# 88 instead of 96 gathered tokens in an expert layer: the last 24 in groups of 16 and 8, 40 tokens' gate table on chip

## The chip, the core and the metric

The kernel runs on one core of a Trainium2 chip, in one launch. The metric is device time in microseconds (us), the median of three runs. A core has a matrix engine (PE, with its weight loads shown apart as PEld), a vector engine (DVE), an activation engine (ACT), GpSimd (POOL) and SyncE (SP). SP, ACT and POOL each issue transfers on a queue of their own, and all queues are served by the same 16 DMA engines.

## The reference, cut to what matters

Two blocks of a network run over 256 tokens of 2048 channels in float32. The change touches the last part, a layer of 16384 experts with one hidden neuron each:

```python
def peer(h, w_q, sub_keys, u_tab, v_tab):          # u_tab, v_tab: 16384 x 2048
    q = (xb @ w_q).reshape(tokens, 8, 2, 128)
    s = einsum('thcd,hcnd->thcn', q, sub_keys)
    ...                                            # 8 heads, 16 experts each
    expert, gates = top16_of_pair_sums(s), softmax(best)
    u_sel, v_sel = u_tab[expert], v_tab[expert]
    act = gelu(einsum('td,thkd->thk', xb, u_sel))
    return einsum('thk,thkd->td', gates * act, v_sel)
```

Behind it come a residual addition and a normalization of each token's row. Each token uses 128 of the 16384 experts.

## The kernel before

**Two ways for the experts.** The 256 tokens are split. 160 tokens go *densely* through all experts: 128 tiles of 128 experts, 1 MB of `u` and 1 MB of `v` a tile. A u-step (`u_step`, products on L1517) multiplies 16 pieces of a u tile with the tokens' columns, 128x160 each, and ACT stores the gelu (L1520). A v-step (`v_step`, `v_products`, L1534) adds 16 products of the v tile with these activations to sums that stay in the accumulator banks 2 to 7. Each float32 product is two instructions on PE, so that a step is 32 of them. The other 96 tokens go *sparsely*: three groups of 32 tokens are spread over the 128 partitions in four quarters (a quarter holds 32 of a token's 128 experts), and an indirect DMA on POOL (`gather`, L1388) fetches one expert's row per partition, 1 MB a gather, 192 gathers in all. On DVE a u item (L1416) multiplies the rows with the tokens (`x_rep`) and sums them; ACT makes the gelu of four such sums at a time (L1434); a v item (L1431) adds the weighted rows to `acc_s`. The quarters are written to DRAM (`sd`), read back and added at the end.

**Order.** 58 u-steps come first, then v-steps and u-steps in turn (70 of each), then 58 v-steps, of which the last two are done by banks, with the closing normalization. The dense tiles come through a ring of five buffers (with three more at its start); SP loads a tile as soon as a buffer is free. The gathers have a ring of five buffers, too, and POOL issues the next when DVE has used one. The program text is written step by step, and each engine follows it in order: after each step `run_paced` adds 0.82 sparse items to the text (`pace`). Each engine may run ahead of the others as far as data and buffers allow. Three things tie them: ACT's gelu of four sparse sums stands in ACT's order between the evacuations of u-steps; the loads of `xq` (`xd` in DRAM to the buffers 20 and 21, L1568 to L1571) stand in POOL's order behind the last u-step, which still reads these buffers; and `weigh` on DVE (L1366, L1369) puts the gates on a tile's activations up to two v-steps ahead.

**The gates.** While the last u-steps run, `gbuild` makes the table of gates for the dense tokens, four tokens at a time (L1350, four products of 128x128). Blocks of 16 tokens are written to DRAM (`gd`, eight blocks), two stay on chip (`kept`). `gload` brings the gates of 16 expert tiles back at a time, 1 MB.

**Handing out.** When the first 128 tokens' choice is known, `hand_out(0)` spreads the expert numbers over the partitions (`rbuf`, L1237), `sp_start` starts the first five gathers, and `hand_out(1)` spreads the gates.

## Time and profile before

| | us |
|---|---|
| median of three runs | 2521.33 |
| lowest, highest | 2519.53, 2522.07 |
| the profiled execution, its own time | 2517.49 |
| span of its trace, first to last instruction | 2515.5 |
| PE, PEld, DVE, ACT, POOL busy | 2395.5, 2268.2, 1604.3, 696.9, 663.0 |
| mean granted clock of PE | 0.99 |

The expert layer takes the last 1290 us of the span. The times of a row are us from the span's start; a busy PE is not PE at its peak, since its instructions overlap.

### The profile page before, as it was taken

How to read it: one execution, taken by the hardware profiler on the slowest of the kernel's cores; microseconds unless marked ns; L12 is line 12 of the kernel's file. 1: busy time of each engine (PE TensorE's matmuls, PEld its weight loads, DVE VectorE, ACT ScalarE, POOL GpSimd, SP SyncE). 2: the span in 40 equal slices, each digit the busy share in tenths (PEclk: the TensorE clock that was granted, in tenths of full speed). 3: DMA queues.
4: the chain of work that ended last, by engine and by line, in shares of the span. 5: the costliest groups of instructions: out<-in, count | busy, mean ns of one | idle time of the engine just before them, and what ended most of it. 6: DMA issues, size and time to landing. Idle time of an engine off the chain costs nothing.

```text
span 2515.5 us, 40335 instructions
## 1 busy us (share of the span) xinstructions
PE 2395.5 (95%) x16832; PEld 2268.2 (90%) x16832; DVE 1604.3 (64%) x2643; ACT 696.9 (28%) x1043; POOL 663.0 (26%) x855
## 2 busy tenths in 40 slices
PE   8999999999999999999999998999999899999997
PEld 7888888899999999988999998988988889999886
DVE  6857777589999987657778675434454343425433
ACT  5544454443335345454211560000000000000002
POOL 1788888410000000140121113212112232121110
PEclk9999999999999999999999999999999999999998
DMA  6455555565555544555599999999999999999994
GB/s 238 168 200 185 176 193 201 203 240 213 198 203 184 185 168 170 187 213 183 217 384 420 420 391 361 413 391 421 417 421 417 385 422 417 390 367 420 418 370 159
DMA packets 110997, 737.76 MB, mean 293 GB/s; under 512 B 13248, under 2 KB 15456, under 8 KB 25280
## 3 DMA queue, kind: packets, MB, share of 16 engines
q1 hardware_dynamic: 65760, 474.50, 49.6%
q0 software_dynamic: 36064, 237.62, 23.7%
q10 hardware_dynamic: 8992, 23.07, 2.5%
q8 instruction: 132, 2.16, 0.3%
q14 instruction: 49, 0.40, 0.0%
HBM read 704.90 MB, written 27.00 MB: 291 GB/s over the span
## 4 chain that ended last, share of the span: by engine, by line
PE 69%; DMA 25%; DVE 4%; ACT 1%; issue 0%; SPq 0%; DVEq 0%; ACTq 0%
DMA s<-in_vexp_dram 14%; PE b L1517 14%; PE b L293 14%; PE b L1534 11%; DMA s<-in_wst_dram 9%; PE b L294 7%; PE b L278 4%; PE b L280 4%; PE b L279 4%; PE b L271 2%; PE b L423 2%; PE b L270 2%; PE b L269 2%; DVE s L195 2%; PE b L1350 1%; PE b L897 1%
## 5 line engine op out<-in xcount | busy, mean ns | idle before, releaser
L1534 PE MATMUL b<-s,s 128*128 128x160 f32 x4096 | 585.2, 303 | 49.7 <-DMA s<-in_vexp_dram 37.3
L1534 PEld LDWEIGHTS b<-s,s 128*128 128x128 f32 x4096 | 566.1, 192 | 66.2 <-issue 49.9
L1517 PE MATMUL b<-s,s 128*128 128x160 f32 x4096 | 584.0, 301 | 27.5 <-DMA s<-in_wst_dram 25.0
L1517 PEld LDWEIGHTS b<-s,s 128*128 128x128 f32 x4096 | 563.5, 191 | 40.0 <-issue 35.9
L293 PE MATMUL b<-s,s 128*128 128x512 f32 x1680 | 597.9, 399 | 0.0
L294 PE MATMUL b<-s,s 128*128 128x256 f32 x1680 | 471.7, 281 | 9.1 <-DVE s L195 9.0
L195 DVE TENSOR_TENSOR s<-s,s 128x2048 fp32r<-128x2048 f32 x192 | 452.3, 2358 | 26.8 <-issue 12.5
L293 PEld LDWEIGHTS b<-s,s 128*128 128x128 f32 x1680 | 315.9, 188 | 71.4
L1416 DVE CUSTOM_DVE_ANT_0 s<-s,s 128x2048 f32<-128x2048 f32 x96 | 219.7, 2290 | 251.5 <-DMA s<-in_uexp_dram,rbuf 224.6
L189 ACT ACTIVATE s<-s 128x2048 fp32r<-128x2048 f32 x192 | 365.7, 1906 | 9.9 <-DMA s<-in_wst_dram 9.9
L294 PEld LDWEIGHTS b<-s,s 128*128 128x128 f32 x1680 | 317.7, 189 | 13.3 <-DVE s L195 12.5
L1431 DVE SCALAR_TENSOR_TENSOR s<-s,sqsum,s 128x2048 f32<-128x2048 f32 x93 | 218.5, 2349 | 164.1 <-DMA s<-in_vexp_dram,rbuf 163.6
L1520 ACT ACTIVATE s<-b 128x160 f32<-128x160 f32 x128 | 38.4, 300 | 825.3 <-PE b L1517 819.6
L278 PE MATMUL b<-s,s 128*128 128x256 f32 x896 | 256.6, 286 | 0.0
L280 PE MATMUL b<-s,s 128*128 128x256 f32 x896 | 253.6, 283 | 0.0
L279 PE MATMUL b<-s,s 128*128 128x256 f32 x896 | 253.5, 283 | 0.0
L1388 POOL DMA_INDIRECT s<-in_uexp_dram,rbuf x96 | 119.8, 1248 | 393.0 <-DVE s L1431 237.2
L1388 POOL DMA_INDIRECT s<-in_vexp_dram,rbuf x96 | 110.2, 1148 | 411.8 <-DVE sqsum L1416 269.6
L278 PEld LDWEIGHTS b<-s,s 128*128 128x128 f32 x896 | 171.8, 192 | 3.7 <-issue 2.9
L279 PEld LDWEIGHTS b<-s,s 128*128 128x128 f32 x896 | 171.9, 192 | 0.3
L280 PEld LDWEIGHTS b<-s,s 128*128 128x128 f32 x896 | 171.9, 192 | 0.0
L837 POOL TENSOR_TENSOR sqsum<-sqsum,s 128x256 f32<-128x256 f32 x28 | 57.9, 2066 | 385.6 <-ACT s L835 385.5
(303 smaller groups left out, 2461.9 us busy)
## 6 DMA issues: line engine op xcount, KB each, us to landing
s<-in_wst_dram SPq DMA_DIRECT2D x320, 1024.0 KB, 5.3
s<-in_vexp_dram SPq DMA_DIRECT2D x128, 1024.0 KB, 19.1
tabd<-s POOLq DMA_DIRECT2D x32, 256.0 KB, 4.7
s<-tabd ACTq DMA_DIRECT2D x32, 256.0 KB, 3.5
gd<-s ACTq DMA_DIRECT2D x8, 1024.0 KB, 11.4
s<-gd POOLq DMA_DIRECT2D x6, 1024.0 KB, 28.9
xd<-s POOLq DMA_DIRECT2D x4, 1024.0 KB, 9.8
s<-in_bblk_dram ACTq DMA_DIRECT2D x8, 512.0 KB, 4.0
```

What stands on the lines that cost most here:

```text
L189: nc.scalar.activation(hi_of(i), raw_of(i), AF.Copy)
L195: nc.vector.tensor_tensor(out=lo_of(i), in0=raw_of(i), in1=FV(hi_of(i)), op=ALU.subtract)
L278: nc.tensor.matmul(ps, a, xh, start=(j == 0), stop=False)
L279: nc.tensor.matmul(ps, a, xl, start=False, stop=False)
L280: nc.tensor.matmul(ps, b, xh, start=False, stop=(j == len(perm) - 1))
L293: nc.tensor.matmul(ps, a, x2, start=(j == 0), stop=False)
L294: nc.tensor.matmul(ps[:, :T], b, x2[:, :T], start=False, stop=(j == len(perm) - 1))
L1388: nc.gpsimd.indirect_dma_start(out=gb[m % len(gb)][0:n, :], out_offset=None, in_=uexp if kind == "u" else vexp, in_offset=bass.IndirectOff ...
L1416: V.tensor_tensor_reduce(out=buf, in0=buf, in1=x_rep[0:4 * n, :], scale=1.0, scalar=0.0, op0=ALU.mult, op1=ALU.add, accum_out=dots_[:, k:k ...
L1431: V.scalar_tensor_tensor(out=ac, in0=buf, scalar=a, in1=ac, op0=ALU.mult, op1=ALU.add)
L1517: nc.tensor.matmul(ps, raw[:, k * P:(k + 1) * P], nv(k)[:, NS_:T], start=(k == 0), stop=(k == KT - 1))
L1534: nc.tensor.matmul(acc[d], raw[:, d * P:(d + 1) * P], act_at(i), start=False, stop=(i == P - 1 and (d % 3 == 2 or d == KT - 1)))
```

## The change

Eight tokens move from the gathered to the dense way: 88 are gathered, 168 are dense. The gathered tokens are now in groups of 32, 32, 16 and 8, all on 128 partitions: a token of the third group has eight parts of 16 experts, one of the fourth sixteen parts of 8, so that the last groups take 32 and 16 gathers; in all there are 176. `pace` is 0.78. The dense products are 128x168. The gate table has 42 pieces of four tokens; eight blocks still go to DRAM, and 16, 16 and 8 tokens stay on chip, so that `weigh` has three small products in place of two.

The parts of the last two groups are no longer written to DRAM: `join_rows` multiplies `acc_s` with a matrix of ones and zeros (`sel`) on PE, four products of 512 columns a group in two pairs, into the banks 0 and 1, and DVE adds them to the residual rows, which are read early (`y_rows`). The numbers and gates of these groups go over a small list in DRAM (`li16`, `li8`), since a token's experts now spread over more partitions. The gathers start after the first group's numbers are handed out.

```diff
 NEG = -1e30
-GROUPS = [(0, 32), (32, 32), (64, 32)]
-NS_ = 96
+GROUPS = [(0, 32), (32, 32), (64, 16), (80, 8)]
+NS_ = 88
 NT = T - NS_
...
         self.paced = []
-        self.pace, self.paced_credit = 0.82 * 2350, 0
+        self.pace, self.paced_credit = 0.78 * 2350, 0
         self.credit = 0
...
     xrow = drp.tile([NS_, D], F32, name="xrow")
-    sd = drp.tile([4, NS_, D], F32, name="sd")
-    NSP = NT // 16 - 2
+    sd = drp.tile([4, 64, D], F32, name="sd")
+    lists = [drp.tile([P, 2, n], F32, name=f"li{n}") for _, n in GROUPS[2:]]
+    NSP = 8
+    STAY = [16, 16, 8]
+    assert 16 * NSP + sum(STAY) == NT
     gd = drp.tile([NSP, P, P, 16], F32, name="gd")
...
             V.tensor_copy(abr[:, P:2 * P], flat(gat))
-        for g, (t0, n) in enumerate(GROUPS):
-            for q in range(4):
-                nc.gpsimd.dma_start(rbuf[n * q:n * q + n, 64 * g + 32 * c:64 * g + 32 * c + 32],
-                                    abr[t0:t0 + n, P * c + 32 * q:P * c + 32 * q + 32])
-        if c == 0:
-            sp_start()
+        for g in range(2):
+            hand_to(c, g)
+            if c == 0 and g == 0:
+                sp_start()
+        for g in range(2, len(GROUPS)):
+            hand_to(c, g)
+    def hand_to(c, g):
+        t0, n = GROUPS[g]
+        Q = P // n
+        K = P // Q
+        dst = rbuf[:, LCOL[g] + c * K:LCOL[g] + c * K + K]
+        if g < 2:
+            for q in range(Q):
+                nc.gpsimd.dma_start(dst[n * q:n * q + n], abr[t0:t0 + n, P * c + K * q:P * c + K * q + K])
+            return
+        li = lists[g - 2]
+        nc.gpsimd.dma_start(li.rearrange("(q t) c k -> t c q k", t=n)[:, c],
+                            abr[t0:t0 + n, P * c:P * c + P].rearrange("p (q k) -> p q k", q=Q))
+        nc.gpsimd.dma_start(dst, li[:, c])
...
+    def by_expert(n):
+        return stage(n).rearrange("p (i t) -> p i t", i=P)
     def gbuild():
-        kept.extend(slots([9]) + [stg[0]])
+        kept.extend(slots([9]) + [stg[0], S[24][:, 0:8 * P]])
         for t4 in range(NT // 4):
...
         n = t4 // 4
-        sg = stage(n).rearrange("p (i t) -> p t i", t=16)
+        sg = by_expert(n).rearrange("p i t -> p t i")
         for q in range(4):
...
         if t4 % 4 == 3 and n < NSP:
-            nc.scalar.dma_start(gd[n], stage(n).rearrange("p (i t) -> p i t", t=16))
+            nc.scalar.dma_start(gd[n], by_expert(n))
...
         nc.vector.tensor_tensor(out=a3, in0=a3, in1=gblk(i // 16)[:, :, i % 16, :], op=ALU.mult)
-        for n in range(2):
-            r = a[:, 16 * (NSP + n):16 * (NSP + n) + 16]
-            nc.vector.tensor_tensor(out=r, in0=r, in1=kept[n][:, 16 * i:16 * i + 16], op=ALU.mult)
+        t0 = 16 * NSP
+        for n, w in enumerate(STAY):
+            r = a[:, t0:t0 + w]
+            nc.vector.tensor_tensor(out=r, in0=r, in1=by_expert(NSP + n)[:, i, :], op=ALU.mult)
+            t0 += w
         if i % 16 == 15 and i // 16 + 2 < 8:
...
+    batches = [(g, k) for g, (_, n) in enumerate(GROUPS) for k in range(0, n, 4)]
     items = []
-    for j in range(8 * len(GROUPS) + 1):
-        for kind, n in (("u", j), ("v", j - 1)):
-            if 0 <= n < 8 * len(GROUPS):
-                items += [(kind, n // 8, n % 8 * 4 + k) for k in range(4)]
+    for j in range(len(batches) + 1):
+        for kind, m in (("u", j), ("v", j - 1)):
+            if 0 <= m < len(batches):
+                items += [(kind, batches[m][0], batches[m][1] + k) for k in range(4)]
     gb = []
+    DCOL = [0, 32, 64, 80]
...
         kind, g, k = items[m]
-        n = 4 * GROUPS[g][1]
         nc.gpsimd.indirect_dma_start(
-            out=gb[m % len(gb)][0:n, :], out_offset=None, in_=uexp if kind == "u" else vexp,
-            in_offset=bass.IndirectOffsetOnAxis(ap=gaddr[0:n, 64 * g + k:64 * g + k + 1], axis=0))
+            out=gb[m % len(gb)][:], out_offset=None, in_=uexp if kind == "u" else vexp,
+            in_offset=bass.IndirectOffsetOnAxis(ap=gaddr[:, LCOL[g] + k:LCOL[g] + k + 1], axis=0))
...
         t0, n = GROUPS[g]
-        for q in range(4):
+        for q in range(P // n):
             nc.gpsimd.dma_start(x_rep[n * q:n * q + n, :], S[18][t0:t0 + n, :])
...
             yield None
-        late = []
+        V.memset(sel, 0.0)
+        for g, (t0, n) in list(enumerate(GROUPS))[2:]:
+            V.tensor_reduce(out=sel[:, 96 * (g - 2) + t0:96 * (g - 2) + t0 + n],
+                            in_=ident.rearrange("p (q t) -> p t q", t=n), axis=AX.X, op=ALU.add)
+        late, sums = [], []
+        acc_s = None
         for m, (kind, g, k) in enumerate(items):
             t0, n = GROUPS[g]
-            buf = gb[m % len(gb)][0:4 * n, :]
-            dots_, acts = dots[0:4 * n, 32 * g:32 * g + 32], dots[0:4 * n, P + 32 * g:P + 32 * g + 32]
+            buf = gb[m % len(gb)]
+            dots_, acts = [dots[:, o + DCOL[g]:o + DCOL[g] + n] for o in (0, P)]
             if kind == "u":
-                V.tensor_tensor_reduce(out=buf, in0=buf, in1=x_rep[0:4 * n, :], scale=1.0, scalar=0.0,
+                V.tensor_tensor_reduce(out=buf, in0=buf, in1=x_rep, scale=1.0, scalar=0.0,
                                        op0=ALU.mult, op1=ALU.add, accum_out=dots_[:, k:k + 1])
...
                 if k % 4 == 0:
-                    a4 = acts[:, k:k + 4]
-                    V.tensor_tensor(out=a4, in0=a4, in1=rbuf[0:4 * n, 64 * g + 32 + k:64 * g + 36 + k], op=ALU.mult)
+                    a4, o = acts[:, k:k + 4], LCOL[g] + n + k
+                    V.tensor_tensor(out=a4, in0=a4, in1=rbuf[:, o:o + 4], op=ALU.mult)
                 if g == 0 and k == 0:
                     acc_s = slots([10])[0]
-                ac = acc_s[0:4 * n, :]
                 if k == 0:
-                    V.tensor_scalar(ac, buf, a, None, op0=ALU.mult)
+                    V.tensor_scalar(acc_s, buf, a, None, op0=ALU.mult)
                 else:
-                    V.scalar_tensor_tensor(out=ac, in0=buf, scalar=a, in1=ac, op0=ALU.mult, op1=ALU.add)
+                    V.scalar_tensor_tensor(out=acc_s, in0=buf, scalar=a, in1=acc_s, op0=ALU.mult, op1=ALU.add)
             while late and m >= late[0][0]:
...
                 gather(m + len(gb))
-            if kind == "u" and k == 31 and g < len(GROUPS) - 1:
+            if kind == "u" and k == n - 1 and g < len(GROUPS) - 1:
                 rows(g + 1)
-            if kind == "v" and k == 31:
-                for q in range(4):
-                    nc.gpsimd.dma_start(sd[q, t0:t0 + n, :], acc_s[n * q:n * q + n, :])
+            if kind == "v" and k == n - 1:
+                if g < 2:
+                    for q in range(4):
+                        nc.gpsimd.dma_start(sd[q, t0:t0 + n, :], acc_s[n * q:n * q + n, :])
+                else:
+                    sums.append((m + 3, g))
+            if sums and m == sums[0][0]:
+                yield 2350
+                yield from join_rows(sums.pop(0)[1], acc_s)
             yield 2350
-        parts = [s[0:NS_, :] for s in gb]
+        y = y_rows[0]
+        quarters = [gb[q][0:64, :] for q in range(4)]
         for q in range(4):
-            nc.gpsimd.dma_start(parts[q], sd[q])
-        nc.gpsimd.dma_start(parts[4], xrow)
-        for _ in range(5):
+            nc.gpsimd.dma_start(quarters[q], sd[q])
+        for _ in range(3):
             yield None
-        for q in range(1, 5):
-            V.tensor_tensor(out=parts[0], in0=parts[0], in1=parts[q], op=ALU.add)
+        yield from join_rows(sums.pop(0)[1], acc_s)
+        for q in range(4):
+            V.tensor_tensor(out=y[0:64, :], in0=y[0:64, :], in1=quarters[q], op=ALU.add)
             yield 2350
...
         c = small[0:NS_, 40:50]
-        nc.scalar.activation(parts[1], parts[0], AF.Square, accum_out=c[:, 0:1])
-        V.tensor_tensor(out=parts[0], in0=parts[0], in1=gf[0:NS_, :], op=ALU.mult)
+        nc.scalar.activation(gb[0][0:NS_, :], y, AF.Square, accum_out=c[:, 0:1])
+        V.tensor_tensor(out=y, in0=y, in1=gf[0:NS_, :], op=ALU.mult)
         yield 2350
...
         yield None
-        nc.scalar.activation(parts[0], parts[0], AF.Copy, scale=c[:, 3:4])
-        nc.gpsimd.dma_start(out[0:NS_, :], parts[0])
+        nc.scalar.activation(y, y, AF.Copy, scale=c[:, 3:4])
+        nc.gpsimd.dma_start(out[0:NS_, :], y)
+    sel, u_done = rconv, [False]
+    y_rows = []
+    def join_rows(g, acc_s):
+        t0, n = GROUPS[g]
+        assert u_done[0]
+        if not y_rows:
+            y_rows.append(slots([18])[0][0:NS_, :])
+            nc.gpsimd.dma_start(y_rows[0], xrow)
+        s_ = sel[:, 96 * (g - 2):96 * (g - 2) + NS_]
+        for h in range(2):
+            for c in range(2):
+                nc.tensor.matmul(B[c][0:NS_, :], s_, acc_s[:, (2 * h + c) * 512:(2 * h + c + 1) * 512],
+                                 start=True, stop=True)
+            yield None
+            for c in range(2):
+                r = y_rows[0][64:NS_, (2 * h + c) * 512:(2 * h + c + 1) * 512]
+                nc.vector.tensor_tensor(out=r, in0=r, in1=B[c][64:NS_, :], op=ALU.add)
+            yield 1400
```

POOL before, behind the first gathers of the start (`rbuf` holds numbers and gates by partition): the gates of all three groups are handed out in 12 transfers, and the gathers go on.

```order
L1388 DMA s_11237<-in_uexp_dram,rbuf 128x2048
L1388 DMA s_11238<-in_uexp_dram,rbuf 128x2048
L1237 DMA rbuf<-s_10073 32x32 x12
L1388 DMA s_11234<-in_uexp_dram,rbuf 128x2048
L1388 DMA s_11235<-in_uexp_dram,rbuf 128x2048
L1388 DMA s_11236<-in_uexp_dram,rbuf 128x2048
```

The same place in the change (L1413 is the gather; `li_10085` and `li_10086` are the lists):

```order
L1413 DMA s_11232<-in_uexp_dram,rbuf 128x2048
L1254 DMA rbuf<-s_10073 32x32 x4
L1257 DMA li_10085<-s_10073 16x8x16
L1259 DMA rbuf<-li_10085 128x16
L1257 DMA li_10086<-s_10073 8x16x8
L1259 DMA rbuf<-li_10086 128x8
L1254 DMA rbuf<-s_10073 32x32 x8
L1257 DMA li_10085<-s_10073 16x8x16
L1259 DMA rbuf<-li_10085 128x16
L1257 DMA li_10086<-s_10073 8x16x8
L1259 DMA rbuf<-li_10086 128x8
L1413 DMA s_11228<-in_uexp_dram,rbuf 128x2048
```

Four lists now stand between the fifth and the sixth gather, each read back right behind its write. Over the whole of POOL's order 42 gathers stood ahead of the instruction that opens the dense sums, 115 between it and the `xq` loads, and 35 behind these; now they are 41, 109 and 26.

PE before, at a v-step of the last stretch (`b_67` to `b_72` are the banks of the dense sums, `s_10972` activations, `s_80` and `s_10975` tiles of v):

```order
L1534 MATMUL b_72<-s_10972,s_80 128x160
L1534 MATMUL b_67<-s_10972,s_10975 128x160 x3
L1534 MATMUL b_68<-s_10972,s_10975 128x160 x3
L1534 MATMUL b_69<-s_10972,s_10975 128x160 x3
L1534 MATMUL b_70<-s_10972,s_10975 128x160 x3
L1534 MATMUL b_71<-s_10972,s_10975 128x160 x3
L1534 MATMUL b_72<-s_10972,s_10975 128x160
```

In the change, behind the 100th v-step (`s_11660` is `acc_s`, `rconv` holds `sel`):

```order
L1591 MATMUL b_72<-s_10974,s_10978 128x168
L1513 MATMUL b_65<-s_11660,rconv 88x512
L1513 MATMUL b_66<-s_11660,rconv 88x512
L1591 MATMUL b_67<-s_10974,s_78 128x168 x3
L1591 MATMUL b_68<-s_10974,s_78 128x168 x3
L1591 MATMUL b_69<-s_10974,s_78 128x168 x3
L1591 MATMUL b_70<-s_10974,s_78 128x168 x3
L1591 MATMUL b_71<-s_10974,s_78 128x168 x3
L1591 MATMUL b_72<-s_10974,s_78 128x168
L1513 MATMUL b_65<-s_11660,rconv 88x512
L1513 MATMUL b_66<-s_11660,rconv 88x512
```

The products of the join stand between v-steps, a pair behind the 100th and a pair behind the 101st; the last group's stand behind the 118th and 119th. DVE's order has the additions behind 167 of the 176 sparse items, and the second join behind all of them.

## Rows read from the trace of the kernel before

**Rows 1.** The page: the span, and GB/s in its 40 equal slices.

```profile
span 2515.5 us, 40335 instructions
...
GB/s 238 168 200 185 176 193 201 203 240 213 198 203 184 185 168 170 187 213 183 217 384 420 420 391 361 413 391 421 417 421 417 385 422 417 390 367 420 418 370 159
```

**Rows 2.** Stages of the expert layer: us, busy us (instructions), PE clock, DMA share, GB/s.

```profile
core 0: us, PE busy (x) PEld busy (x) DVE busy (x) ACT busy (x) POOL busy (x), PEclk, DMA share, GB/s
1225.20:1397.60 172.40, 169.67 (x1240) 167.78 (x1239) 124.64 (x380) 22.61 (x62) 38.12 (x53) 1.00 0.88 349
1397.60:1515.20 117.60, 117.60 (x923) 117.60 (x922) 93.80 (x180) 73.28 (x138) 22.12 (x18) 1.00 0.98 396
1515.20:1531.90 16.70, 5.46 (x39) 5.08 (x37) 0.56 (x4) 0.55 (x2) 0.38 (x1) 0.81 1.03 403
1531.90:2163.00 631.10, 586.17 (x4111) 566.00 (x4112) 292.16 (x404) 20.63 (x77) 161.56 (x135) 0.99 1.01 409
2163.00:2216.30 53.30, 51.63 (x374) 50.57 (x373) 13.93 (x25) 1.61 (x6) 2.34 (x3) 1.00 0.89 340
2216.30:2285.80 69.50, 69.50 (x514) 69.50 (x513) 27.52 (x51) 0.60 (x3) 15.28 (x16) 1.00 1.01 407
2285.80:2418.40 132.60, 122.63 (x865) 117.71 (x863) 68.78 (x128) 2.10 (x5) 21.76 (x23) 1.00 1.01 419
```

**Rows 3.** The chain that ended last: start us, us, engine, line, count.

```profile
1230.44 43.47 PE b L1517 x320
...
1400.74 2.17 PE b L1517 x16
1403.81 2.18 PE b L1517 x16
...
1632.35 24.22 DMA s<-in_vexp_dram
...
2216.26 69.56 PE b L1534 x512
...
2457.89 32.60 PE b L1534 x216
```

**Rows 4.** POOL in order of time: start us, us, line, in brackets idle before and releaser.

```profile
1265.82 0.94 POOL L1388 DMA_INDIRECT s<-in_uexp_dram,rbuf  x1 [3.25 <-DMA s<-in_uexp_dram,rbuf]
...
1298.69 0.99 POOL L1388 DMA_INDIRECT s<-in_uexp_dram,rbuf  x1 [0.60 <-DMA rbuf<-s]
...
1562.34 0.94 POOL L1388 DMA_INDIRECT s<-in_vexp_dram,rbuf  x1 [4.03 <-DVE sqsum L1416]
1567.33 0.94 POOL L1388 DMA_INDIRECT s<-in_vexp_dram,rbuf  x1 [4.05 <-DVE sqsum L1416]
...
2214.39 0.94 POOL L1568 DMA_DIRECT2D s<-xd  x1 [50.58 <-PE b L1517]
...
2217.85 1.01 POOL L1388 DMA_INDIRECT s<-in_uexp_dram,rbuf  x1 [0.30 <-issue]
...
2394.91 0.95 POOL L1388 DMA_INDIRECT s<-in_vexp_dram,rbuf  x1 [4.04 <-DVE s L1431]
```

**Rows 5.** DMA from 1531.9 to 2216.3: packets, MB, mean rate; issues, KB, us to landing.

```profile
DMA packets 38997, 275.96 MB, mean 403 GB/s; under 512 B 4397, under 2 KB 4895, under 8 KB 5928
...
s<-in_vexp_dram,rbuf POOLq DMA_INDIRECT x58, 22.3
```

**Rows 6.** Gathers issued (POOL's instructions on L1388) by stage, columns as in rows 2.

```profile
1531.90:2163.00 631.10, 149.45 (x115) 0.99 1.01 409
...
2216.30:2418.40 202.10, 33.56 (x35) 1.00 1.01 415
```

**Rows 7.** Groups by line: busy us, mean ns, idle before; waits from 1531.9 to 2163.

```profile
L1416 DVE CUSTOM_DVE_ANT_0 s<-s,s 128x2048 f32<-128x2048 f32 x96 | 219.7, 2290 | 251.5 <-DMA s<-in_uexp_dram,rbuf 224.6 <-DMA s<-s 27.0
L1369 DVE TENSOR_TENSOR s<-s,s 128x16 f32<-128x16 f32 x256 | 32.3, 167 | 0.0
...
DVE sqsum L1424 <- ACT sqsum L1434: 65.4, 5, 21.2
```

**Rows 8.** DMA issues of the whole span: KB each, median us to landing.

```profile
rbuf<-s POOLq DMA_DIRECT2D x24, 4.0 KB, 4.7
```

6 lines of the change are left out of this document (4 added, 2 removed).

## The prediction, made before the run

> **What bounds the kernel now.** The page comes first: the transfer rate doubles halfway, from about 200 GB/s to about 420, and stays there [rows 1]. That half is the expert layer. The view by stages tells what it consists of [rows 2]. Up to 1515.2 there are u-steps alone, and PE is busy in 287.3 of 290.0 us: PE is the bound. At 1515.2 comes a stop of 16.7 us for the gate table. From 1531.9 to 2163.0, the long stage, v- and u-steps alternate with DMA at 409 GB/s and PE busy in 586 of 631 us. Then follow 53.3 us in which PE hardly waits and DMA falls to 340, and the v-steps alone.
>
> The chain of waits gives the price of a step [rows 3]. Ten u-steps (320 instructions) without a wait took 43.47 us and sixteen v-steps 69.56, both 4.347 a step. In the long stage 4111 instructions, 128.5 steps, took 631.1 us, 4.91 a step: 0.56 is lost at each, in stretches such as the 24.22 us of one tile's transfer in the chain. What the tiles wait for shows in POOL's order of time [rows 4]: gathers go out every 4.99 us. A gather and a dense tile are 1.05 MB each, so that a pair in 4.99 us is 420 GB/s, the whole rate: gathers and tiles share it, while both are queued. The gathers also run ahead of PE, until POOL stands for 50.58 us at the `xq` loads, which wait for the last u-step. PE then runs at its own speed. After that 35 gathers follow, to 2394.91 [rows 4, 6].
>
> So PE and DMA are both close to their limits here, and the change takes from one to give to the other.
>
> **A step on PE.** A product of 160 columns costs 4347/32 = 135.8 ns per instruction. Between two runs of 16 such instructions 3.07 us pass, of which 2.18 are the run; the 0.89 left are eight instructions of the gate table with 128 columns, 111 ns each [rows 3]. On that line (0.77 ns a column) 168 columns take 142.0 ns; in proportion to 160 columns, 142.6. The step becomes 4.54 to 4.56; I take 4.55, +0.205. For all 256 steps that is +52 us where PE is the bound.
>
> The weight loads are a second reading: PEld is busy in all of the 69.5 us in which PE is [rows 2], so they could be what sets 135.8. The same weight loads kept a spacing of 111 ns beside 128 columns, so the columns set it. The Trainium skill ("Perfetto Trace Analysis", Identifying the Most-Contended Engine) takes the busy share of the weight loads as the measure of the matrix engine. By that rule wider products would cost nothing here; the spacing at 128 columns speaks against it.
>
> **Up to 1531.9.** 58 u-steps: 58 x 0.205 = +11.9. Two more pieces of the table: 2 x 0.89 = +1.8. Of the 2.7 us of idle time some 1.7 go, since slower steps ask for tiles less often. Sum **+12** (+10 to +15). The stop of 16.7 us stays: as before, eight blocks go to DRAM and one megabyte must come back before the first v-step.
>
> The handing out gets longer on POOL. The sixth gather went out 32.9 us after the fifth [rows 4]. In the change four lists are written and read back in order, each with two landings in turn; a small transfer lands in 4.7 us [rows 8], so up to 8 x 4.7 = 38 us more, and nothing at the least, if they pass while the first five gathers are still in flight anyway. I take 20 us later and no cost: a gap in the gathers gives the tiles the whole rate, and DVE has to be 36 and not 37 items on at the first v-step. What stands behind it is under the rivals.
>
> **1531.9 to 2216.3**, 684.4 us, 140 steps. PE alone needs 140 x 4.347 = 608.6, in the change 140 x 4.55 = 637. DMA moved 275.96 MB [rows 5]; with 109 gathers for 115 [rows 6], as the order of the change has them, it is 6.3 MB less, 269.7. How far the gathers run ahead decides the rest. DVE cannot pass ACT's gelus by more than 7 items (a gelu stands two items behind its four sums, its v items seven later), and five gathers are in flight: 12 items, 12/0.78 = 15 steps of 4.55, 70 us. DVE did wait for these gelus, 65.4 us [rows 7], so that the limit was touched. The stop at the `xq` loads then takes 70 us in place of 53.3. It moved 53.3 x 0.340 = 18.1 MB; the 16.7 us more carry tiles alone at 1.05/4.55 = 0.230 MB/us, 3.8 MB. The other 247.8 MB at 409 GB/s take 606 us. Together 676, **-8**.
>
> The bounds: if every gather costs its tile's share of time as now, the loss of 684.4 - 608.6 = 75.8 us over 123 megabytes on POOL's queue becomes 75.8 x 117/123 x (4.99 - 4.55)/(4.99 - 4.35) = 50, and 637 + 50 = 687, +2. If the stop grows no longer, 251.6/0.409 + 53.3 = 668, -16. If the rings hide all of it, PE's 637 and the 18 us that DMA loses at the stop and with the slow reads of the table, 655, -29.
>
> **From 2216.3 to the end**, 299.2 us, 58 v-steps. +11.9 for these. Eight join products of 512 columns: 512 x 0.77 + 12 = 406 ns per instruction, two each, **+6.5**. PE does not wait at them: from `xq` to the first join are 30 steps, 137 us, and DVE needs 21 sparse items with 17 gathers and some 3 MB of other transfers, 20 x 4.99 = 100 us. DVE waits there instead, which holds back the last gathers by some 35 us and gives the tiles the rate. PE's waits were 2490.5 (2457.89 + 32.60) [rows 3] less 2216.3 less 252.1 = 22 us; with 26 for 35 gathers, 2 for 4 MB read back and a smaller deficit per step I take 7, -15. The closing transposes have 40 rows for 32 and 504 columns for 480, +1. Sum **+4** (+1 to +10).
>
> **At nothing:** DVE loses 16 items of 2.29 us and gains 128 small products of 0.167 [rows 7], 21 us, beside idle time of more than half the long stage (292 of 631 busy) [rows 2]. `sel` is a handful of small operations. The first two groups' sums are still written and read as before.
>
> **Sum:** 12 - 8 + 4 = **+8**. The profiled execution took 2517.5 for a span of 2515.5, so 2525.5 now; it was 3.8 below the median. On the median, 2521.3 + 8 = **2529**.
>
> **Rivals.**
> *The bytes decide (faster).* 16.8 MB of gathers less are 40 us at 420 GB/s. It holds if the rings even out gathers and tiles so that PE waits for neither: 655 in the middle (-29), no waits at the end (-3), +10 ahead: 2499. For it: 0.56 us a step are lost to transfers today. Against it: 52 us of PE work come in their place, and the stop leaves DMA unused. It decides once the middle falls below 668. Chance 0.15.
> *Half the rate while a gather is queued (slower).* The 4.99 us for both kinds of transfer say that a queued gather takes half. Then pace and run-ahead do not matter: +12, +2, and at the end the 22 us of waits become 22 x 31/38 x 0.44/0.64 = 12, so 11.9 + 6.5 - 10 + 1 = +9; 2544. The Trainium skill ("DMA: Bandwidth & Descriptors", Queues, rings and completion order) says that each DMA engine takes turns between the queues that have work, a packet at a time; by that rule this is the case that comes. Against it: a ring of five tiles can fill in each short pause of the gathers. Chance 0.15.
> *The lists hold PE.* If the second batch of dots comes after ACT's gelu in the order, ACT holds the evacuation of a u-step and PE with it: up to the 20 to 38 us of delay less the two steps (9 us) of slack, +11 or more: 2540 and above. Chance 0.08.
> *Weight loads set the step.* Then nothing is added per step: +2, -16 and -5: 2502. Chance 0.05.
>
> The forecast keeps 0.57. A run of this kernel can be told from no change beyond 0.2%, 5 us; of the 0.57 I put 0.22 within (2516 to 2526) and 0.35 above. Faster: 0.15 + 0.05 = 0.20. Same: 0.22. Slower: 0.35 + 0.15 + 0.08 = 0.58. The range 2508 to 2548 leaves out most of the bytes and weight-load cases and the worst of the lists, under 0.2.
>
> **What would show it.** Sixteen v-steps without a wait at 72.8 us (69.6 if the weight loads set it). The first v-step some 12 us later, behind a stop as long as before. POOL's wait at the `xq` loads near 65 us and more DVE time on ACT's gelus; 140 steps in 676 us. Few waits of PE for tiles after that, DVE waiting for the first join for some 30 us, no wait of PE at a join. I am wrong if PE waits at the joins, if the middle keeps its loss per step, or if it sheds nearly all of it.

## The result, and the profile after

| | before | after |
|---|---|---|
| median of 5 runs each, us | 2521.33 | 2534.66 |
| range, us | 2519.53 to 2525.51 | 2533.28 to 2537.71 |
| ratio, 95% interval | | 1.0053, 1.0038 to 1.0068 |
| profiled execution: span, us | 2515.5 | 2531.4 |

The change makes the kernel 13.3 us slower, and the interval lies clear of 1. The forecast was 8 us. The three stretches of the sum, in the span of the two profiled executions: up to the first v-step, from there to POOL's first load of `xq`, and from there to the end.

| us | before | after | difference | predicted |
|---|---|---|---|---|
| up to the first v-step | 1531.9 | 1543.4 | +11.5 | +12 |
| the middle | 682.5 | 669.5 | -13.0 | -8 |
| the end | 301.1 | 318.5 | +17.4 | +4 |

Before's marks are in [rows 2, 4], after's below. The differences add up to +15.9, that of the two profiled spans. The prediction and the expectations of the runs part the middle from the end where the last u-step ends, 2216.3 before and 2215.2 after: there the differences are -12.6 and +17.0, and the 672 and 316 us of the expectations are the 669.5 and 318.5 of these tables. The first term holds, the second lies within its bounds, the third is far off. The page of the kernel after, the span and GB/s in 40 slices, as in [rows 1]:

```profile
span 2531.4 us, 40516 instructions
GB/s 235 170 199 183 181 188 208 205 229 213 206 202 183 176 175 169 189 206 198 215 365 420 409 356 360 421 387 421 417 421 413 402 387 413 358 382 393 298 304 117
```

The last six slices are lower than before's: 358 382 393 298 304 117, where before had 390 367 420 418 370 159. The stages of the layer after, columns as in [rows 2]:

```profile
1225.90:1401.60 175.70, 175.70 (x1240) 175.70 (x1240) 122.88 (x382) 22.90 (x62) 39.68 (x52) 1.00 0.86 337
1525.00:1543.40 18.40, 5.98 (x39) 5.29 (x37) 2.71 (x6) 0.53 (x2) 4.06 (x4) 0.78 0.96 371
1543.40:2172.00 628.60, 612.92 (x4181) 600.70 (x4182) 283.68 (x463) 21.45 (x78) 155.04 (x132) 0.99 1.00 407
2172.00:2215.20 43.20, 43.20 (x305) 43.20 (x304) 15.24 (x40) 1.50 (x6) 2.60 (x4) 1.00 0.85 327
2215.20:2342.00 126.80, 125.89 (x875) 124.53 (x874) 49.30 (x113) 0.56 (x4) 31.51 (x41) 1.00 1.01 388
2342.00:2392.00 50.00, 30.55 (x180) 26.93 (x179) 11.86 (x39) 1.69 (x3) 5.35 (x4) 0.80 0.72 265
```

In the long stage PE is busy in 612.9 of 628.6 us, where it was 586 of 631. The new thing is the last row: 50 us in which PE works for 30.6 and the transfers stand at 265 GB/s. The chain of waits shows what stands there (start us, us, what):

```profile
1231.33 45.60 PE b L1574 x320
1543.35 7.57 PE b L1591 x32
2238.13 31.17 DMA s<-s
2269.58 9.73 DMA s<-s
2342.76 36.17 DMA s<-xrow
2379.77 3.71 PE b L1513 x4
2383.49 76.59 PE b L1591 x531
```

Ten steps take 45.60 us, 4.56 a step, as forecast. `s<-s` are the loads of the last group's rows, L1420; `s<-xrow` is the load of the residual rows at the first join, which landed 36.17 us after POOL issued it. PE stood for it ahead of the second pair of the join, and that pair took 3.71 us, where the other pairs take 1.72. The waits from 2215.2 on (who waited for whom: us in total, times, longest):

```profile
DVE s L1518 <- DMA s<-xrow: 36.1, 1, 36.1
PE b L1513 <- DVE s L1518: 19.4, 1, 19.4
PE b L1591 <- DMA s<-in_vexp_dram: 0.6, 3, 0.3
```

PE hardly waits for a tile any more; but for 4.6 us at the closing transposes (4.7 before), all of its waiting is at the join. Before, in the same view from 2214.4 on, it waited for tiles:

```profile
PE b L1534 <- DMA s<-in_vexp_dram: 16.6, 25, 3.1
```

POOL in time, columns as in [rows 4]:

```profile
2172.61 1.01 POOL L1413 DMA_INDIRECT s<-in_uexp_dram,rbuf  x1 [14.70 <-DVE s L1460]
2212.88 0.95 POOL L1626 DMA_DIRECT2D s<-xd  x1 [39.27 <-PE b L1574]
...
2237.18 0.94 POOL L1413 DMA_INDIRECT s<-in_uexp_dram,rbuf  x1 [3.97 <-DVE sqsum L1446]
2238.13 1.12 POOL L1420 DMA_DIRECT2D s<-s  x2
...
2268.32 0.52 POOL L1420 DMA_DIRECT2D s<-s  x1 [5.38 <-DMA s<-in_uexp_dram,rbuf]
...
2280.10 1.01 POOL L1413 DMA_INDIRECT s<-in_uexp_dram,rbuf  x1 [1.42 <-DMA s<-s]
...
2342.76 0.58 POOL L1509 DMA_DIRECT2D s<-xrow  x1
2387.69 1.72 POOL L1413 DMA_INDIRECT s<-in_vexp_dram,rbuf  x1 [44.34 <-DVE sqsum L1446]
```

Two holes in the gathers: from 2237.2 to 2280.1, while POOL issues the sixteen row loads one by one, each behind an older transfer, and from 2342.8 to 2387.7, while the join waits. Before, a gather went out every 4.99 us in such a stretch. In the first hole and just behind it, from 2238 to 2290, the view of transfers gives:

```profile
DMA packets 3040, 18.56 MB, mean 357 GB/s; under 512 B 650, under 2 KB 650, under 8 KB 906
...
s<-s POOLq DMA_DIRECT2D x16, 64.0 KB
s<-in_uexp_dram,rbuf POOLq DMA_INDIRECT x4
```

357 GB/s at a busy share of 1.01: the engines count as busy all the time and move 15% less than the 420 of the 52 us behind it. With tiles alone, from 2195 to 2212, the share was 0.65 at 226 GB/s, so a low rate need not come with a full share.

**The theories.** The first one is that the end's loss is the wait at the join (19.4 us), which comes of POOL's queue. Its rival is that the end is short of transfers, through the row loads, and a wait that is taken away at one place comes back at another as a wait for tiles. Other questions for the runs: whether the wider steps cost anything behind the first v-step, whether the lists do, and what sets the middle.

### The profile page after: what moved, and what is told of

Its sections match the earlier page's. It is cut to its first block, busy times and chain, and to the rows that moved or that the text cites. A ratio compares the mean times of both kernels' runs of the same rounds, so it can differ in the third digit from the quotient of the medians.

```text
span 2531.4 us, 40516 instructions
## 1 busy us (share of the span) xinstructions
PE 2439.8 (96%) x16864; PEld 2320.7 (92%) x16864; DVE 1584.4 (63%) x2764; ACT 701.4 (28%) x1047; POOL 665.0 (26%) x855
## 4 chain that ended last, share of the span: by engine, by line
PE 77%; DMA 16%; DVE 4%; ACT 1%; issue 1%; POOL 0%; SPq 0%; DVEq 0%; POOLq 0%; ACTq 0%
PE b L1574 19%; PE b L293 13%; PE b L1591 13%; PE b L294 7%; DMA s<-in_vexp_dram 6%; PE b L278 4%; PE b L280 4%; PE b L279 4%; DMA s<-in_wst_dram 4%; DVE s L195 2%; PE b L423 2%; PE b L271 2%; PE b L270 2%; PE b L269 2%; DMA s<-s 2%; DMA s<-in_uexp_dram,rbuf 2%
## 5 line engine op out<-in xcount | busy, mean ns | idle before, releaser
L1591 PE MATMUL b<-s,s 128*128 128x168 f32 x4096 | 605.5, 308 | 21.4 <-DVE s L1392 12.1
L1591 PEld LDWEIGHTS b<-s,s 128*128 128x128 f32 x4096 | 591.9, 191 | 31.8 <-issue 19.1
L1574 PE MATMUL b<-s,s 128*128 128x168 f32 x4096 | 604.7, 307 | 7.3 <-DMA s<-in_wst_dram 6.8
L1574 PEld LDWEIGHTS b<-s,s 128*128 128x128 f32 x4096 | 586.9, 190 | 13.5 <-issue 13.2
L195 DVE TENSOR_TENSOR s<-s,s 128x2048 fp32r<-128x2048 f32 x192 | 454.1, 2367 | 27.3 <-issue 12.3
L293 PEld LDWEIGHTS b<-s,s 128*128 128x128 f32 x1680 | 316.1, 188 | 72.5
L1446 DVE CUSTOM_DVE_ANT_0 s<-s,s 128x2048 f32<-128x2048 f32 x88 | 201.3, 2290 | 249.8 <-DMA s<-in_uexp_dram,rbuf 202.7
L294 PEld LDWEIGHTS b<-s,s 128*128 128x128 f32 x1680 | 317.6, 189 | 12.4 <-DVE s L195 11.7
L1577 ACT ACTIVATE s<-b 128x168 f32<-128x168 f32 x128 | 39.4, 308 | 812.8 <-PE b L1574 792.5
L1460 DVE SCALAR_TENSOR_TENSOR s<-s,sqsum,s 128x2048 f32<-128x2048 f32 x84 | 197.4, 2350 | 78.1 <-DMA s<-in_vexp_dram,rbuf 77.1
L1413 POOL DMA_INDIRECT s<-in_uexp_dram,rbuf x88 | 115.0, 1307 | 364.1 <-DVE s L1460 192.9
L1413 POOL DMA_INDIRECT s<-in_vexp_dram,rbuf x88 | 105.4, 1197 | 387.2 <-DVE sqsum L1446 289.1
L278 PEld LDWEIGHTS b<-s,s 128*128 128x128 f32 x896 | 171.8, 192 | 3.7 <-issue 2.9
L279 PEld LDWEIGHTS b<-s,s 128*128 128x128 f32 x896 | 171.9, 192 | 0.3
L280 PEld LDWEIGHTS b<-s,s 128*128 128x128 f32 x896 | 171.8, 192 | 0.0
```

What stands on the lines that cost most here:

```text
L195: nc.vector.tensor_tensor(out=lo_of(i), in0=raw_of(i), in1=FV(hi_of(i)), op=ALU.subtract)
L278: nc.tensor.matmul(ps, a, xh, start=(j == 0), stop=False)
L279: nc.tensor.matmul(ps, a, xl, start=False, stop=False)
L280: nc.tensor.matmul(ps, b, xh, start=False, stop=(j == len(perm) - 1))
L293: nc.tensor.matmul(ps, a, x2, start=(j == 0), stop=False)
L294: nc.tensor.matmul(ps[:, :T], b, x2[:, :T], start=False, stop=(j == len(perm) - 1))
```

## The experiments

Each ratio is to the kernel before, in the same session, where its median was 2519.38 (first four runs), 2519.81 (next four) and 2519.06 (last four). The stretches are of the profiled execution: the first v-step, POOL's first `xq` load and the end of the span mark them off as above, and PE's waits are those from the `xq` load on, from the view of waits (for tiles + for the join). Every kernel also waits some 4.6 us at the closing transposes, those with pace 0.74 17. Where the program is the same, the stretches show their scatter: the change, ACT's load, no joins and one join with the rows as they were lie within 2.8 us at the first v-step and 1.1 in the middle; the kernels with two groups spread and pace 0.78 lie within 2.9 in the middle, and those with spread rows, one join and pace 0.78 within 1.6 at the end.

| kernel | median us | ratio (95%) | first v-step | middle | end | PE's waits in the end |
|---|---|---|---|---|---|---|
| before | 2521.3 | 1 | 1531.9 | 682.5 | 301.1 | 16.6 + 0 |
| the change | 2534.7 | 1.0053 (1.0038 to 1.0068) | 1543.4 | 669.5 | 318.5 | 0.6 + 19.4 |
| ACT loads the residual | 2529.2 | 1.0036 (1.0023 to 1.0050) | 1541.2 | 669.8 | 312.4 | 12.1 + 0 |
| 160 columns | 2524.6 | 1.0025 (1.0016 to 1.0034) | 1534.8 | 666.5 | 319.4 | 9.8 + 18.5 |
| late read-back | 2536.5 | 1.0061 (1.0047 to 1.0075) | 1543.3 | 669.6 | 320.2 | 3.2 + 17.9 |
| pace 0.82 | 2538.9 | 1.0072 (1.0058 to 1.0085) | 1542.8 | 690.8 | 305.1 | 0 + 9.0 |
| no joins | 2527.2 | 1.0035 (1.0021 to 1.0049) | 1544.0 | 669.8 | 310.9 | 15.1 + 0 |
| spread rows, one join | 2523.1 | 1.0013 (1.0004 to 1.0022) | 1552.0 | 663.5 | 302.8 | 4.6 + 0 |
| the same, pace 0.74 | 2527.7 | 1.0034 (1.0023 to 1.0045) | 1551.0 | 655.9 | 319.0 | 6.2 + 0 |
| the change, pace 0.74 | 2530.9 | 1.0043 (1.0029 to 1.0056) | 1539.4 | 663.3 | 326.4 | 4.8 + 5.7 |
| early spread, one join | 2523.3 | 1.0016 (1.0004 to 1.0028) | 1559.0 | 664.7 | 301.5 | 4.5 + 0 |
| early spread, two joins | 2522.5 | 1.0013 (0.9997 to 1.0029) | 1560.4 | 666.4 | 303.0 | 0 + 6.2 |
| one join, rows as they were | 2527.8 | 1.0034 (1.0022 to 1.0047) | 1543.7 | 668.7 | 311.2 | 9.0 + 0 |
| three groups spread | 2522.1 | 1.0011 (1.0001 to 1.0021) | 1555.6 | 660.0 | 301.2 | 4.4 + 0 |

**The residual load on ACT's queue.** In `join_rows`:

```
-            nc.gpsimd.dma_start(y_rows[0], xrow)
+            nc.scalar.dma_start(y_rows[0], xrow)
```

> The load of the residual rows for the join is issued by ACT instead of POOL, so that it no longer stands behind the gathers in POOL's queue. Theory A (PE's wait of 19.4 us at the second pair of the first join is the wait for these rows, which land 36.2 us after their issue): the wait goes, with 1 to 3 us of slower steps behind it: 2513 to 2517, a ratio of 0.996 to 0.998 to the kernel before. Rival B (DVE reaches the join too late anyway, since the sixteen row loads of the last group hold POOL for 40 us): PE still waits some 10 us or more, 2524 to 2535. Rival C (the last gathers become the bound behind it): 2525 to 2530.

The wait at the join is gone, yet the end shrinks by 6.1 us only, and the time is not the 2513 to 2517 of the first theory. ACT issued the load at 2307.2, some 36 us earlier than POOL had, so that this run changes the queue and the time of issue together. The chain of this kernel, from 2213 to the end, shows where the rest went:

```profile
2213.05 59.29 PE b L1591 x416
2272.36 18.48 DMA s<-in_vexp_dram
...
2295.80 25.93 DMA s<-in_vexp_dram
...
2401.31 24.99 DMA s<-in_vexp_dram
```

PE waits for tiles behind the pieces of 2272 and 2296, at and after the row loads, and again behind that of 2401.

**Steps of 160 columns.** Leaves out the products of the last eight dense tokens but for the first piece of each u-step; all else stays.

```
+                w = NT if k == 0 else 160
-                nc.tensor.matmul(ps, raw[:, k * P:(k + 1) * P], nv(k)[:, NS_:T], ...
+                nc.tensor.matmul(ps[:, :w], raw[:, k * P:(k + 1) * P], nv(k)[:, NS_:NS_ + w], ...
...
-            nc.tensor.matmul(acc[d], raw[:, d * P:(d + 1) * P], act_at(i), start=False,
+            nc.tensor.matmul(acc[d][:, :160], raw[:, d * P:(d + 1) * P], act_at(i)[:, :160], start=False,
```

> Leaves out the products of the last 8 dense tokens (but for the first of the 16 pieces of a u tile): steps of 160 columns as before, all else as in the change. Theory A (the middle is limited by bytes while gathers run, and by PE's step only where it has caught up): 11 us less ahead of the first v-step, the middle from 671.8 us to 660 to 666, the end 10 us less: 2503 to 2510. Rival B (half the rate while a gather is queued): the middle does not get shorter, 672 to 681: 2513 to 2523. Rival C (PE's step is all that counts): 52 us less, 2483.

Eight v-steps without a wait in one piece of its chain, 256 instructions of L1592, and the join's load:

```profile
2332.72 35.76 DMA s<-xrow
2373.03 34.80 PE b L1592 x256
```

34.80/8 = 4.35: the step is that of before. It gains 8.6 us ahead of the first v-step, 3.0 in the middle, and loses 0.9 at the end, where the theory had 10 less; so the time is 2524.6 and not 2503 to 2510. The 42 us of wider products behind the first v-step (198 steps at 0.21) cost hardly anything in the change: PE only does in them what it would else have waited. And the end loses its 18 us against before without any wider step.

**The lists' read-back issued later.** In the handing out the two reads of each list are kept in a list of their own and issued at item 16.

```
-        nc.gpsimd.dma_start(dst, li[:, c])
+        later.append((dst, li[:, c]))
...
+            if m == 16:
+                for d_, s_ in later:
+                    nc.gpsimd.dma_start(d_, s_)
```

> The four reads of the lists back into the partitions are issued behind the 17th sparse item and no longer hold POOL between the fifth and the sixth gather, where it waited 27.9 us for the lists' writes. Theory A (the later gathers of the start cost nothing, as another 18 us at the first v-step go to the gate table): 2531 to 2537, no change. Rival B (the late start makes the gathers lag into the middle): up to 10 us less, 2525.

POOL's wait of 27.9 us for the list writes is gone (what it still waits at the lists, 8.9 us, is for gathers), and nothing else moves: all three stretches are within 2 us of the change's. The lists cost nothing in the change as it stands.

**Pace 0.82** in place of 0.78: `self.pace, self.paced_credit = 0.82 * 2350, 0`.

> Only pace, 0.82 in place of 0.78. Theory A (DVE is held by ACT's gelus in the middle, so that the program's share of gathers per step sets the transfers there): about 5 more gathers fall ahead of the xq loads and as many fewer behind; the middle gets 5 to 10 us longer, the join comes 5 steps earlier but its rows as late, 2530 to 2545. Rival B (the gathers run at the rate that DMA gives, whatever pace says): the middle as before within 2 us, 2532 to 2537.

More gathers fall into the middle and fewer into the end (19 behind the `xq` load for 26). The middle takes 21.3 us more, where 5 to 10 were expected, and the end 13.4 less. The sixteen row loads now stand ahead of the `xq` loads (2174.8 to 2208.9), so that they leave the end, too: it has no wait for tiles, and 9.0 us at the join.

**No joins.** The eight products and the additions of `join_rows` left out; the residual rows are loaded and stored.

> Leaves out the eight products and the additions that join the last two groups' partial rows into the residual rows; the output lacks those sums; the residual rows are still loaded and stored. Theory A (the joins and the wait for the residual rows, whose load lands 36.2 us after POOL issues it, are most of what the end lost): the four pairs' 6.9 us, the 19.4 us wait of PE at the first join and some microseconds of the lower clock behind it go; the end falls from 316 to 290 to 303 us, and the time by 14 to 20 us, to 2515 to 2520. Rival (the end is bound by its own transfers, and a wait only changes its place): the tile waits grow by as much, as they did when ACT issued the residual load; the end stays at 308 or more and the time at 2527 or more.

The first theory asked for an end of 290 to 303 and got 308.6 by its mark, 310.9 in the table. Its chain, from 2213 to the end:

```profile
2238.25 30.84 DMA s<-in_uexp_dram,rbuf
2269.38 9.47 DMA s<-s
2279.13 11.59 DMA s<-s
...
2298.28 19.89 DMA s<-in_vexp_dram
...
2357.45 24.82 DMA s<-in_vexp_dram
...
2402.59 28.39 DMA s<-in_vexp_dram
```

With no join at all PE waits 15.1 us for tiles. The theory of the join falls: the wait there is real, but behind it stands a shortage of transfers which costs nearly as much wherever it shows. All that the end gains without the joins is 7.6 us, about their own products (6.9).

**Spread rows and one join.** The rows of groups 2 and 3 are laid out over 128 partitions in DRAM by 24 small transfers of SP in the u-steps 10 to 33, and loaded in one transfer each; the last group has an accumulator of its own, and both are joined at the very end; POOL loads the residual rows behind the `xq` loads.

```
+        if g >= 2:
+            nc.gpsimd.dma_start(x_rep, spread[g - 2])
+            return
         for q in range(P // n):
...
+                if g == 3 and k == 0:
+                    acc2, acc_s = acc_s, slots([15])[0]
...
+        if 10 <= i < 34:
+            g, q = (2, i - 10) if i < 18 else (3, i - 18)
+            t0, n = GROUPS[g]
+            nc.sync.dma_start(spread[g - 2][n * q:n * q + n, :], S[18][t0:t0 + n, :])
```

> The last two groups' rows are spread over the 128 partitions in DRAM ahead of time by 24 small transfers of SP under the first steps, and loaded in one transfer each; the last group has an accumulator of its own, and both groups are joined once at the very end, two products a bank, four additions; POOL loads the residual rows right behind the loads of the tokens' rows. Theory A: the row loads' pause of some 42 us, the 19.4 us wait and half of the additions go; the middle stays at 672, the end falls from 316 to about 302, a tail some 4 us longer included: 2518 to 2523, ratio to before 0.998 to 1.001. Rival (the end is bound by its transfers): no better than with ACT issuing the residual load, about 2527 to 2530.

The end is 302.8, about what this version was expected to have; the middle, expected to stay, is 6.0 less. The time, 2523.1, is at the upper bound of what was expected. But the small transfers stand between tiles in SP's queue, at a time when PE is the bound. Two pieces of its chain where the change has 109.44 us of u-steps in one:

```profile
1355.86 19.61 DMA s<-in_wst_dram
1375.53 23.12 DMA s<-in_wst_dram
```

The first v-step comes 8.6 us later than in the change.

**The same with pace 0.74**, and **the change with pace 0.74 alone**.

> As the run with the spread rows and one join, with the pace at 0.74 in place of 0.78. Theory A (the pace decides how many gathers lie in the middle, and the end has room for more of them once the joins do not stop it): the middle falls from 672 to 652 to 657, the end grows by less than 10 us: 2503 to 2514. Rival (the transfers are only moved to the end, which then waits for them): the end gives back 15 us or more, and the time is within 4 us of the run at 0.78.

> The change with the pace at 0.74 in place of 0.78 and nothing else. Theory A: the middle falls by 15 to 20 us as with the spread rows, but the later gathers push row loads, residual load and join further into the end, so that the end grows by 5 to 20: 2520 to 2535. Rival (the joins do not matter and only the pace does): the same gain as between the two runs with spread rows, so 15 to 20 us below the change, 2515 to 2520.

The middle falls by 7.6 us to 655.9 and by 6.2 to 663.3, and the end gives back 16.2 and 7.9 us. With spread rows that is the rival's case, though the time, 4.6 us above that at 0.78, is a little more than it allowed; without them the gain in the middle is short of the 15 to 20 that were expected. In the spread version PE is busy in nearly all of that middle, and then the sparse work is late. Its stage row, columns as in [rows 2]:

```profile
1551.00:2208.80 657.80, 649.95 (x4481) 643.35 (x4482) 283.39 (x487) 22.53 (x81) 170.05 (x122) 0.99 0.99 400
```

Two of the waits from 2208 on:

```profile
PE b L1674 <- DVE s L1667: 17.1, 5, 12.9
PE b L1588 <- DMA s<-in_vexp_dram: 6.2, 21, 1.4
```

PE's closing transposes (L1674) wait 17.1 us for DVE, most of it once, behind a last gather at 2394; without the spread rows it is 16.9. The pace shifts gathers between two stretches that are both full. With spread rows 0.74 is slower than 0.78; of the change itself these intervals tell neither 0.74 nor 0.82 from it.

**The spread alone, early, with ACT issuing.** The 24 small transfers go out on ACT's queue in the u-steps 2 to 9, three a step. With one join, with the change's two joins, and with a third group spread; and one join without any spread.

```
+        for m in range(3 * i - 6, min(3 * i - 3, 24)) if i > 1 else ():
+            g, q = (2, m) if m < 8 else (3, m - 8)
+            t0, n = GROUPS[g]
+            nc.scalar.dma_start(spread[g - 2][n * q:n * q + n, :], S[18][t0:t0 + n, :])
```

> As the run with the spread rows and one join at pace 0.78, but ACT issues the 24 small transfers under the u-steps 2 to 9, where the transfer rate was near nothing at 1230 to 1240. From its first v-step that run took 966 us against 988 of the change, and it lost 8.6 us ahead of it to tiles that came late behind the small transfers. If their place was the whole of that loss, the first v-step comes back to 1543 and the time is 2510 to 2515, ratio to before 0.996 to 0.998. If two megabytes more in that stage cost the tiles as much wherever they are issued, 2518 to 2523.

> The change with the early spread of the last two groups' rows alone; its two joins and POOL's load of the residual rows stay. Theory B (the 24 row loads from 16 and 8 partitions cost the end and the middle: they run the transfers at 300 to 350 GB/s in place of 420 and hold the gathers behind them): the middle falls by 4 to 6 us and the end by 6 to 10, and the wait at the first join stays at some 19 us: 2520 to 2526. Rival (the joins' order makes the gain of the spread version): no gain, 2531 to 2535.

> The change with one join of both groups at the end and POOL's early load of the residual rows; the row loads stay as in the change. Theory B: the wait at the first join goes, the tile waits behind the row loads stay and grow, as they did without any join: 2526 to 2531. Rival (the joins' order makes the gain): 2515 to 2522.

> As the early spread with one join, with the second group's rows spread too (four loads from 32 partitions become one from 128). Theory B: a row load from fewer partitions costs the rate also here: in the middle the stretch with that group's loads moved 400 GB/s where the next ones moved 419, 2 MB in 100 us, 4.5 us; so 2 to 5 us below the run with two groups spread. Rival (32 partitions are as good as 128 and the rate was lost to other small transfers): within 2 us of it.

In the run with one join and the rows as they were, the slot of the tokens' rows is taken for the residual rows before the last group's loads read it, so that the last group's sums are of other numbers; its transfers are the change's in number and size.

The run with the change's own two joins settles the end: with the row loads alone replaced, it takes 303.0 in place of 318.5, with the same 26 gathers behind the `xq` load. Its POOL in time:

```profile
2251.44 0.61 POOL L1421 DMA_DIRECT2D s<-sp  x1
2255.61 0.97 POOL L1414 DMA_INDIRECT s<-in_uexp_dram,rbuf  x1 [3.56 <-DVE s L1464]
2260.59 0.94 POOL L1414 DMA_INDIRECT s<-in_uexp_dram,rbuf  x1 [4.00 <-DVE s L1464]
```

The gather behind the row load goes out 4.2 us after it, not 42. Its chain, and its wait at the join:

```profile
2228.72 136.80 PE b L1595 x960
2365.52 1.72 PE b L1517 x4
...
PE b L1517 <- DVE s L1522: 6.2, 1, 6.2
```

Thirty v-steps follow one another without a wait, up to the first join. And the transfers from 2250 to 2302, against those of the change from 2238 to 2290:

```profile
DMA packets 3106, 21.69 MB, mean 417 GB/s; under 512 B 334, under 2 KB 334, under 8 KB 590
```

21.7 MB pass in 52 us for 18.6, with three gathers more. At the join, with the residual load still on POOL's queue, PE waits 6.2 us and not 19, since DVE gets there sooner. The two kernels with one join and spread rows have about the same end (302.8, 301.5), so the place of the join adds little once the rows are spread. One join alone, with the rows as they were, gives 311.2, as no join does, and 2527.8 in all, as theory B expected.

The early place was a mistake of its own: the first v-step came later still (1559.0 and 1560.4), and the time of the version with one join stayed at 2523.3, at the edge of what was expected for the case that two megabytes cost the tiles as much wherever they are issued. The waits of the run with two joins, up to 1530, show by which way:

```profile
PE b L1578 <- ACT s L1581: 12.3, 3, 10.1
...
ACT sqsum L1467 <- DVE sqsum L1450: 18.4, 1, 18.4
```

ACT stands 18.4 us at its gelu of the sparse dots, and PE stands 12.3 us for the evacuation queued behind it. The dots are late: up to 1530 DVE waits 30.2 us for its first gathers, 13.3 in the change. That the small transfers delay them is the likely reading. The times of this run also spread more than any other's (2511.7 to 2537.3); the profiled execution, at 2531.5, is a long one, and what it loses ahead of the first v-step need not be the median's loss. Its median, 2522.5, is within the 2520 to 2526 of theory B, but of other parts: the end gained 15.5 and not 6 to 10, the middle 3.1 and not 4 to 6. A third group spread lowered the middle by another 4.7 us against the version with two, but by medians the two versions differ by 1.2 us and that is no difference. No version here has a median below that of the kernel before.

## Why the prediction was right, and where it was not

The total came nearer to the forecast than its terms did: the middle was 5 us better and the end 13 us worse than said. That the two errors partly cancel, so that 2534.7 stands beside 2529, is luck.

**Up to the first v-step** (+12, measured +11.5): right in the main, and for the reason given. PE is the bound there and pays 0.21 a step; with 160 columns 8.6 of it come back. Of the 11.5 us, 9.1 are in the u-steps and the gate table; the stop, forecast to stay, is 1.7 longer, and 0.7 lies ahead of the layer.

**A step of 4.55**: 4.56. The weight loads as what sets the step fall with it; they are busy in all of the time in which PE is, before and after, and the spacing still went with the columns.

**The middle** (-8, measured -13.0): the form of the term was right, its parts less so. Bytes over rate describe it, with 269.72 MB as worked out (before 275.96 at 403 GB/s, [rows 5]):

```profile
DMA packets 38207, 269.72 MB, mean 401 GB/s; under 512 B 4368, under 2 KB 4862, under 8 KB 5906
...
DVE sqsum L1454 <- ACT sqsum L1463: 136.7, 10, 26.3
...
2169.78 0.16 DVE L1454 TENSOR_TENSOR sqsum<-sqsum,rbuf 128x4 f32<-128x4 f32 x1 [13.09 <-ACT sqsum L1463]
```

The step that failed is "The stop at the `xq` loads then takes 70 us in place of 53.3": POOL's wait there was 39.3 us, shorter than the 50.6 of before. DVE did wait longer for ACT's gelus (136.7 us for 65.4), but that did not stretch the stop. The last line, and POOL's order above, show why. A gelu that DVE waits for comes once in eight items, so that the lead over PE rises and falls within such a round, and the stop hangs on where in it the last gather ahead of the `xq` loads stands. In the change it goes out 2.8 us after DVE's wait for a gelu (2172.61 after 2169.78), and the stop is what is left up to the last u-step; before, eight gathers went out behind such a gelu, of 2134.2, the last at 2162.9, 51 us ahead of the loads. Nor do the five gathers in flight lengthen it, as the forecast had it: the text puts each gather at the item five before its own. Of the 29 us (140 x 0.21) that the wider steps add on PE here, the middle pays 3, by the run with 160 columns.

**The end** (+4, measured +17.4): here the sum failed. By the prediction's own mark it is +17.0: 12.1 from the steps, 6.9 from four pairs of join products, 1.1 from the close, all near the forecast, and -3.1 from the waits and the slower instructions behind them, where -15 was forecast. These come to 24.4 us in the change and 27.5 before. (The forecast's 22 us are 5.5 short: 40 of the 1856 instructions of these steps stand behind the first closing transpose and were counted in the close as well. The difference hardly feels it.) The step that failed was "PE does not wait at them", on the ground that DVE reaches the join in 20 x 4.99 = 100 us; PE's wait at a join was named as a sign of being wrong, and it came. The count took the row loads into "some 3 MB of other transfers" at the full rate, and gave the time until the residual load lands no term of its own. The sixteen loads kept the gathers away for 42 us and the whole of the transfers at 357 GB/s for 52 us: 52 x (0.417 - 0.357) = 3.1 MB, 7.5 us of transfers. DVE's last item ahead of the join ended at 2341.5, 12 us before PE got there and not 37; then the residual load took another 36.2. DVE does wait at the first join, 36.1 us where some 30 were forecast, but for that load, and PE with it. With the rows loaded in one piece PE waits 6.2 us, near the 7 of the prediction, but at the join and not for tiles, so that this agreement is chance.

Why little is to be had even then: before, 27.5 us of the end were waits and what they slow down. The wider steps, the joins and the longer close put 20.1 us of PE's work in their place, so that with no wait at all the end would be 294 us, 7 under before's 301.1. The best that ran is 301.2. So the six gathers fewer in the middle are worth 13 us there, the nine fewer at the end at most 7, and the 11.5 ahead of them take back most of the former.

**The rivals.** *The bytes decide*: in part. Its 655 us in the middle did not come, nor the 668 below which it was to decide (671.8 by its mark). But the middle does go with the bytes: steps of 160 columns change it by 3 us only, and at pace 0.82, where it takes 21.3 more, 276.3 MB pass in it at 400 GB/s for 269.0 at 402. The end has its own floor, PE's. *Half the rate while a gather is queued* asked for +2 in the middle; the -12.6 measured there speaks against it. *The lists hold PE*: not in the change, where later reads moved nothing; but the mechanism exists, as the early spread showed with 12.3 us of PE waiting for ACT.

**Why the row loads are slow.** Shown is that with sixteen loads of 64 KB from 8 partitions in 52 us, beside eleven megabytes of tiles, the transfers run at 357 GB/s with a busy share of 1.01, and that with one load of the same megabyte from DRAM in their place they run at 417. The Trainium skill ("SBUF — State Buffer", Door 1: The DMA port swizzle) says that the rate of a transfer hangs on how many of the memory's 16 ports its partitions reach; the partitions 80 to 87, on which these rows lie, are on two of the sixteen. The trace agrees with that rule in its direction: 357 for 417 GB/s. No run here parts it from the number of transfers or from where the rows are read, since the spread version changed all three. And few partitions are not the whole of it: in the run with early spread and two joins 246 to 264 GB/s passed from 2366 to 2374, at a share of 1.0, while the residual load to 88 partitions was under way. The pauses between the loads, in which each waits for an older transfer, are part of the 42 us in any case.

What stays open: what the kernel would take with the rows spread at no cost to the u-steps. Added up from these profiles, with the first v-step at 1543, it would be 1543 + 664 + 302 = 2509 in the span against before's 2515.5, but no such kernel was run, and a version whose small transfers came earlier lost more, not less.

## What to carry to other kernels

A wait that heads the list need not be what the time hangs on: when its removal brings tile waits in its place, look for the stretch before it in which the transfers are busy and move little. A row of small loads belongs into such an account with the time for which it holds its queue, not with its bytes. And where two resources are both near their limits, price a trade between them stretch by stretch: here wider steps cost most of their price where PE was the bound and nearly nothing where transfers were, and the bytes saved were worth at most 7 us in the stretch that PE's own work nearly fills.

## What the runs showed of the hardware that was not expected

A load of 704 KB on POOL's queue landed 36.2 us after its issue, behind gathers of a megabyte each that were still under way; the tiles in the chains took 18 to 28. Issued right behind the `xq` loads, in the run with spread rows and one join, it landed after 15.5. The busy share of the transfer engines stood at 1.01 at 357 GB/s as well as at 420, so that it does not tell a full stretch from a slow one. And the pair of products behind the wait at the join took 3.71 us where the others took 1.72, at the lower of TensorE's two levels (1.2 GHz for 2.4). PE had stood still for 19.4 us, and the granted clock, 1.00 up to 2342, was 0.50 here; columns as in [rows 2]:

```profile
2379.70:2383.50 3.80, 3.73 (x5) 1.45 (x6) 1.84 (x7) 0.00 (x0) 0.00 (x0) 0.50 0.01 2
```

Behind 6.2 us of standing, in the run with early spread and two joins, it was 0.50 for that pair, too.
